# Feed-forward weights split by two chunks at a time, outer filter taps scaled on ScalarE, gates and splits for two row tiles at once

## The chip, the core and the metric

The kernel runs on one core of one Trainium2 chip. The core has a matrix engine (TensorE, PE in the profile, with its weight loads as PEld), a vector engine (VectorE, DVE), an engine for activations (ScalarE, ACT), a general engine (GpSimd, POOL) and a queue that issues most transfers (SyncE, SP). Each engine takes its instructions in order. The metric is the time of one execution on the device, in microseconds (us).

## The reference

A trunk of two layers on a sequence of 256 positions with 2048 channels, all in float32. Layer 0 mixes by pooling and attention, layer 1 by an mLSTM. Behind each mixer stands the same gated feed-forward block with 5632 hidden channels, and that block is what the change touches:

```python
def conv_ffn(x, w_up, conv_w, conv_b, w_down):
    u = x @ w_up
    up = jnp.pad(u, ((0, 0), (1, 1), (0, 0)))
    c = conv_w.astype(u.dtype)
    u = c[0] * up[:, :-2] + c[1] * up[:, 1:-1] + c[2] * up[:, 2:] + conv_b.astype(u.dtype)
    gate, val = jnp.split(u, 2, axis=-1)
    return (jax.nn.silu(gate) * val) @ w_down
```

The up product has 2 x 5632 output channels (gate and value), a filter of three taps runs over the positions, and SiLU of the gate times the value goes into the down product.

## The kernel before

**Weights.** Every weight matrix is cut on the host into chunks of 128 partitions by 1024 float32 values (512 KB). The program uses 890 chunks in one fixed order; `Stream` (from line 65) brings them in. `load` (line 82) takes a buffer `w` and issues the chunk's transfer on SP's queue. `split` (line 146) turns it into a pair of float32r values: a cast on ScalarE gives the high part (line 152), a subtraction on VectorE the low part (line 153), both into a buffer `hl`. Each float32 product is then three products of such parts (high x high, high x low, low x high). `ahead` (line 159) keeps loads and splits a set number of chunks in front of the matmuls: 5 and 2 outside the feed-forward blocks, 7 and 3 inside (line 1145), where there are 7 buffers `w` and 5 buffers `hl`. `next` hands out the chunk that the next matmuls use.

**Row tiles.** The 5632 hidden channels are 44 row tiles of 128, in groups of 4, 8, 8, 8, 8 and 8 (`FCH`). A row tile holds gate and value: 2 x 256 positions. Of each group of 8, the first four tiles (and all four of the group of 4) are made by `up` (line 969): four chunks, 16 matmuls each (8 with 512 and 8 with 256 columns). The other four tiles are a unit of `quads` (line 1019), which uses a scheme with fewer products (7 instead of 8 block products): 28 chunks of 6 matmuls (`p`), after which `finish` (line 1074) transposes the sums back (`tr`). The sums of weight blocks that the units need are either made in memory ahead of time by accumulating transfers from GpSimd (`make_step`, tiles `G`) or on VectorE (`sums` of `Stream`, lines 130 to 144).

**The tail of a row tile.** `tail` (line 953) works on gate and value in turn: ScalarE scales the middle tap and adds the bias (line 958), VectorE adds the outer taps with two multiply-adds (lines 959 and 961). Then SiLU on ScalarE (964), the product on VectorE (965), a cast on ScalarE (966) and a subtraction on VectorE (967) leave the split result in `g`, which is what the down product reads. Before that, `up` brings its two halves together (lines 432 and 433) and multiplies by the norm's factor (977); `finish` copies the transposes out (1083).

**Order.** TensorE's instructions stand in the program's order. `_ffn_plan` (line 1240) interleaves one chunk at a time: chunks of `up`, of `down` (line 1116, chunks of 12 matmuls `dn` of the group before), and of the units, spread over the places given in `UNITS`. The last group's `down` stands alone at the end of the layer, behind the `down` of the group before it. Small tasks (`finish`, the sums of activations, the norms) are put in between by `Weave`, which counts an estimated time at every group of matmuls. The other engines are ordered by a planner from dependencies.

Of the kernel before, what the change touches and what calls it, by code (L numbers as in the profile page):

```python
# [9 lines left out]
F32 = mybir.dt.float32  # L10
# [6 lines left out]
P = 128  # L17
# [46 lines left out]

class Stream:


    def __init__(self, tc, wpool, spool, dpool, srcs, make, load_ahead, split_ahead):
        self.tc, self.nc, self.wpool, self.spool, self.srcs = tc, tc.nc, wpool, spool, srcs
# [3 lines left out]
        self.more = None  # L73
        self.made, self.make, self.dpool = {}, make, dpool

    def home(self, i, raw):
        if self.more is None or i >= self.more[2]:
            return self.wpool if raw else self.spool
        return ((self.wpool if i % 7 < 6 else self.more[0]) if raw else
                (self.spool if i % 5 < 4 else self.more[1]))  # L80

    def load(self, pieces=1):
        i = self.n_load
        src = self.srcs[i]
        kind, src = src if isinstance(src, tuple) else ("plain", src)
        w = self.home(i, True).tile([P, CH * P], F32, tag="w", name=f"w{i}")
        if kind in ("made", "have"):
            width = n = CH * P
            at = 0
            for part in src:  # L90
                part = self.made[part[0]][:, part[1] * 512 : part[2] * 512] if isinstance(part, tuple) else part
                to = at + part.shape[-1]
                self.nc.sync.dma_start(w[:, at:to], part)
                at = to
        else:
            width = src.shape[-1]
            n = width // pieces
            for c in range(0, width, n):
                self.nc.sync.dma_start(w[:, c : c + n], src[:, c : c + n])
        self.w[i] = [w, n, width, kind, False]  # L100
        self.n_load += 1
        for step in self.make.pop(i, ()):
            self.make_step(*step)
# [26 lines left out]
    def sums(self, i):  # L130
        if i in self.w and not self.w[i][4] and self.w[i][3] not in ("plain", "made"):
            w, kind = self.w[i][0], self.w[i][3]
# [6 lines left out]
            if kind == "left":  # L139
                pin(add(l, l, r))  # L140
            if kind == "chain":
                pin(add(l, l, self.sum))
                pin(add(r, r, l))
            self.w[i][4] = True

    def split(self, then=None):
        i = self.n_split
        self.sums(i)
        w, n, width = self.w.pop(i)[:3]
        hl = self.home(i, False).tile([P, 2, CH * P], F32R, tag="hl", name=f"hl{i}")  # L150
        for c in range(0, width, n):
            (self.nc.vector.tensor_copy if i + c == 0 else self.nc.scalar.copy)(hl[:, 0, c : c + n], w[:, c : c + n])  # L152
            self.nc.vector.tensor_sub(hl[:, 1, c : c + n], w[:, c : c + n], hl[:, 0, c : c + n].bitcast(F32))  # L153
            then and then(c // n)
        self.hl[i] = hl
        self.n_split += 1
        self.sums(i + 1)

    def ahead(self, i, split=None):
        n = len(self.srcs)  # L160
        while self.n_load < min(n, i + self.la + 1):
            if self.n_load >= self.n_split + self.la - self.sa + 1:
                self.split()
            self.load()
        while self.n_split < min(n, i + (self.sa if split is None else split) + 1):
            self.split()

    def next(self):
        i = self.at
        self.ahead(i)  # L170
        self.at += 1
        return self.hl.pop(i)
# [48 lines left out]
def trunk(ctx: ExitStack, tc: tile.TileContext, gx, xT, xn, call, catt, cml, weights, make, out):  # L221
# [9 lines left out]
    wp = pool("wraw", 6)  # L231
    sp = pool("wsplit", 4)
# [705 lines left out]
    def ffn_layer(layer, norm, nxt):  # L938
        with ExitStack() as es:
# [4 lines left out]
            xsp = cp1 = lp(f"fs{layer}", 1)  # L944

# [7 lines left out]
            def tail(u, f, gt, i):  # L953

                y = tp.tile([P, 2, S], F32, tag="y", name=f"y{layer}_{f}")
                for j in range(2):
                    tl = f + j * FT
                    a.activation(y[:, j, :], u[:, j, :], AF.Identity, scale=cw(tl, 1), bias=cw(tl, 3))
                    v.scalar_tensor_tensor(y[:, j, 1:S], u[:, j, 0 : S - 1], cw(tl, 0), y[:, j, 1:S],
                                           ALU.mult, ALU.add)  # L960
                    v.scalar_tensor_tensor(y[:, j, 0 : S - 1], u[:, j, 1:S], cw(tl, 2), y[:, j, 0 : S - 1],
                                           ALU.mult, ALU.add)
                s_ = y[:, 0, :]
                a.activation(s_, s_, AF.Silu)
                v.tensor_mul(s_, s_, y[:, 1, :])
                a.copy(gt[:, i, 0, :], s_)
                v.tensor_sub(gt[:, i, 1, :], s_, gt[:, i, 0, :].bitcast(F32))

            def up(f, gt, i):
                ps = mmp.tile([P, 2, 2, S], F32, tag="mm", name=f"up{layer}_{f}")  # L970
                for q in range(KT // 4):
                    stat_part(ps, xx, list(range(4 * q, 4 * q + 4)), q == 0, q == KT // 4 - 1)
                    if q < KT // 4 - 1:
# [45 lines left out]
            def quads(fs, c, i0, name):  # L1019
# [9 lines left out]
                for p in range(m):  # L1029
# [9 lines left out]
                    yield  # L1039
# [12 lines left out]
                for p in range(m):  # L1052
# [8 lines left out]
                    yield  # L1061
                    if p % 2:
                        hl = st.next()
                        for n in range(2):
                            product(b1, block_of(2 * (p - 1 + n) + 1, 0), hl, n * 512, False, p - 1 + n == m - 1)
                        if p == m - 1:
                            c11 = part(11)
                            a.activation(c11, b1, AF.Copy, scale=r0)
                            gt = g_of(c)
                            wv.add(finish(c12, c22, fs[2:], gt, i0 + 2, name), 3.0)  # L1070
                            wv.add(finish(c11, c21, fs[:2], gt, i0, name), 11.0)
                        yield

            def finish(top, bottom, fs, gt, i0, name):

                for n, f in enumerate(fs):
# [7 lines left out]
                    tail(u, f, gt, i0 + n)  # L1084
# [31 lines left out]
            def down(c, gt, b):  # L1116
# [6 lines left out]
                for k in range(0, len(kts), 2):  # L1123
                    mov_part(ps, lambda k: gt[:, k], kts[k : k + 2], k == 0, k == len(kts) - 2)
                    if k < len(kts) - 2:
                        yield
# [18 lines left out]
            st.la, st.sa, st.more = 7, 3, (lp(f"fw{layer}", 1), lp(f"fh{layer}", 1), st.at + len(_ffn_plan(layer)))  # L1145
# [17 lines left out]
            st.la, st.sa, st.more = 5, 2, None  # L1163
# [61 lines left out]
def _down_chunks(w):  # L1225
# [9 lines left out]
    ((1, 1, 17, 38, 2), (2, 1, 45, 64, 2), (3, 1, 71, 100, 3), (4, 1, 107, 129, 2), (5, 1, 136, 158, 2)),  # L1235
    ((1, 1, 17, 39, 2), (2, 1, 46, 67, 2), (3, 1, 74, 97, 2), (4, 1, 104, 128, 2), (5, 1, 135, 157, 2)),
# [3 lines left out]
def _ffn_plan(layer):  # L1240

    slots = []
    for c, n in enumerate(FCH):
# [6 lines left out]
        for e in fill:  # L1250
            slots += [e] * (4 if e[0] == "n" else FCH[e[1]] // 2)
    here = [[] for _ in slots]
    m = KT // 2
    for c, h, lo, hi, kind in UNITS[layer]:
        one, two = 2 * m, m + m // 2
        long = 1.25 if kind == 3 else 1.0
        step = (hi - lo - 3) / (one * long + two)
        for k in range(one + two):
            at = k * long if k < one else one * long + k - one
            here[int(lo + at * step + (3 if k >= one else 0))].append(("s", c, h))  # L1260
# [3 lines left out]
    for b in range(NB):  # L1264
        plan += [("d", len(FCH) - 1, b)] * (FCH[-1] // 2)
    return plan

# [14 lines left out]
def _ffn_order(layer, up, dn, four, last):  # L1282
# [4 lines left out]
    for step in _ffn_plan(layer):  # L1287
        kind, c, i = step
        n = pos.get(step, 0)
        pos[step] = n + 1  # L1290
        if kind == "n":
            seq.append(up[(sum(FCH[:c]) + i) * 4 + n])
        elif kind == "d":
            seq.append(dn[d0[c] + i * (FCH[c] // 2) + n])
        else:
            u = [e[:2] for e in UNITS[layer]].index((c, i))
            made = UNITS[layer][u][4]
            if n >= 2 * m and (n - 2 * m) % 3 == 2:
                seq.append(last[u, (n - 2 * m) // 3])
                continue  # L1300
# [133 lines left out]
```

## Time and profile before

| | us |
|---|---|
| three runs | 2163.64, 2163.3, 2160.51 (median 2163.3) |
| the profiled execution, from its first to its last instruction | 2160.9 |
| attention layer | 0 to 266.8 |
| feed-forward of layer 0 | 266.8 to 973.0 |
| mLSTM layer | 973.0 to 1458.8 |
| feed-forward of layer 1 | 1458.8 to 2160.9 |

The stages overlap at their borders: the last down product of a layer begins while small work of the next is already under way, so the borders are those of TensorE's instructions to within a few matmuls. The clock granted to TensorE was 1.000 of full speed. In the profile's rows an engine and a line come first, then the operation, the tiles (written first, then read), the shapes, the count, busy time and mean duration; a group made by a helper carries the helper's line, so all matmuls have line 268 and are told apart by tile.

### The profile page before, as it was taken

The page shows a single profiled execution, that of the slowest core. Times are in us where ns is not written, and L with a number is a line of the kernel's source. Part 1 is how long each engine was busy: PE and PEld are TensorE (multiplying, and loading weights), DVE is VectorE, ACT ScalarE, POOL GpSimd, SP SyncE. Part 2 cuts the span into 40 slices and gives each one's busy share as a digit, 9 for nine tenths or more (in the row PEclk, how much of TensorE's full clock was granted, in tenths as well). Part 3 has the DMA queues.
Part 4 walks back from the last instruction along what each step waited for, and adds up shares of the span by engine and source line. Part 5 has one row for each costly group of instructions (what it writes and reads, how often), then busy time and mean ns, then how long its engine had stood idle before and what let it go on. Part 6 is the DMA issues. An engine that isn't in the chain of part 4 may idle for free.

```text
span 2160.9 us, 31049 instructions
## 1 busy us (share of the span) xinstructions
PE 2153.2 (100%) x10896; PEld 1826.7 (85%) x10896; DVE 1717.8 (79%) x2400; ACT 1309.2 (61%) x1840; POOL 276.0 (13%) x344
## 2 busy tenths in 40 slices
PE   9999999999999999999999999999999999999999
PEld 7888888888888888888888888888888888888887
DVE  7686698989889797866777677669898888879785
ACT  7665566766557576655454544556676666757663
POOL 0122111111111111111111111110000010000000
PEclk9999999999999999999999999999999999999999
DMA  8878899999999999979998998887999999877773
GB/s 325 257 229 246 256 262 345 316 332 320 308 325 308 351 332 339 319 200 250 250 263 251 256 253 244 258 244 223 312 286 306 302 297 288 272 249 238 259 245 119
DMA packets 204702, 596.15 MB, mean 276 GB/s; under 512 B 26010, under 2 KB 28354, under 8 KB 204546
## 3 DMA queue, kind: packets, MB, share of 16 engines
q1 hardware_dynamic: 167776, 531.43, 70.1%
q0 software_dynamic: 33696, 59.00, 18.3%
q10 hardware_dynamic: 3074, 3.75, 0.9%
q8 instruction: 85, 1.39, 0.2%
q14 instruction: 71, 0.58, 0.1%
HBM read 591.93 MB, written 119.58 MB: 329 GB/s over the span
## 4 chain that ended last, share of the span: by engine, by line
PE 93%; DMA 5%; DVE 1%; ACT 0%; issue 0%; SPq 0%; ACTq 0%; DVEq 0%
PE up L268 23%; PE dn L268 20%; PE p L268 16%; PE op L268 8%; PE mo L268 4%; PE mk L268 4%; PE mq L268 4%; PE mv L268 3%; PE qproj L268 3%; PE kproj L268 1%; PE vproj L268 1%; PE tr L1081 1%; DMA w<-G 1%; PE pool L268 1%; DMA w<-in_m_in 1%; DMA w<-in_up 1%
## 5 line engine op out<-in xcount | busy, mean ns | idle before, releaser
L153 DVE TENSOR_TENSOR hl<-w,hl 128x1024 fp32r<-128x1024 f32 (+2 forms) x892 | 1075.6, 1218 | 319.9 <-ACT hl L152 302.0
L152 ACT CAST hl<-w 128x1024 fp32r<-128x1024 f32 (+2 forms) x891 | 924.8, 1048 | 646.9 <-PE up L268 98.9
L268 PE MATMUL up<-xx,hl 128*128 128x512 f32 (+1 forms) x3072 | 560.2, 337 | 0.0
L268 PEld LDWEIGHTS up<-xx,hl 128*128 128x128 f32 x3072 | 486.7, 188 | 76.7
L268 PE MATMUL dn<-hl,g 128*128 128x512 f32 x2064 | 491.8, 391 | 0.0
L268 PEld LDWEIGHTS dn<-hl,g 128*128 128x128 f32 x2064 | 385.1, 188 | 79.0
L268 PE MATMUL p<-hl,sx 128*128 128x512 f32 x960 | 250.6, 390 | 0.0
L124 POOL DMA_DIRECT2D G<-in_q x160 | 132.0, 830 | 875.5 <-DMA G<-in_q 872.4
L268 PEld LDWEIGHTS p<-hl,sx 128*128 128x128 f32 x960 | 176.0, 188 | 34.4 <-DVE hl L153 0.6
L128 POOL DMA_DIRECT2D G<-G x144 | 127.9, 888 | 538.2 <-DMA G<-in_q 243.0
L268 PE MATMUL p<-hl,xx 128*128 128x512 f32 x720 | 193.5, 390 | 0.0
L268 PEld LDWEIGHTS p<-hl,xx 128*128 128x128 f32 x720 | 130.8, 188 | 24.0
L268 PE MATMUL mk<-xx,hl 128*128 128x512 f32 (+1 forms) x512 | 92.5, 338 | 1.4 <-DVE hl L153 1.4
L268 PE MATMUL mq<-xx,hl 128*128 128x512 f32 (+1 forms) x512 | 92.2, 337 | 0.0
L268 PE MATMUL mv<-hl,xx 128*128 128x512 f32 (+2 forms) x480 | 91.8, 350 | 0.0
L268 PE MATMUL op<-hl,cat 128*128 128x512 f32 x384 | 91.6, 393 | 0.0
L268 PE MATMUL mo<-hl,xx 128*128 128x512 f32 x384 | 90.5, 391 | 0.0
L268 PEld LDWEIGHTS mk<-xx,hl 128*128 128x128 f32 x512 | 79.0, 188 | 13.1 <-DVE hl L153 1.8
L268 PE MATMUL op<-hl,mcat 128*128 128x512 f32 x384 | 89.5, 392 | 0.0
L268 PEld LDWEIGHTS mq<-xx,hl 128*128 128x128 f32 x512 | 79.3, 188 | 11.6
L268 PEld LDWEIGHTS mv<-hl,xx 128*128 128x128 f32 x480 | 78.3, 189 | 11.2
L268 PEld LDWEIGHTS op<-hl,mcat 128*128 128x128 f32 x384 | 71.5, 188 | 14.6
(242 smaller groups left out, 1865.2 us busy)
## 6 DMA issues: line engine op xcount, KB each, us to landing
w<-in_up SPq DMA_DIRECT2D x192, 512.0 KB, 6.1
w<-in_dn SPq DMA_DIRECT2D x176, 512.0 KB, 6.2
w<-in_m_in SPq DMA_DIRECT2D x124, 512.0 KB, 6.0
w<-in_q SPq DMA_DIRECT2D x88, 512.0 KB, 6.2
G<-in_q SPq DMA_DIRECT2D x144, 256.0 KB, 6.4
G<-G POOLq DMA_DIRECT2D x144, 256.0 KB, 7.5
w<-G SPq DMA_DIRECT2D x72, 512.0 KB, 6.1
w<-in_a_in SPq DMA_DIRECT2D x46, 512.0 KB, 6.1
```

Of the source, the lines that this page charges most:

```text
L124: pin(add.dma_start(G[r, 0:512], src[r, 512:1024], accum_op=ALU.add))
L128: pin(add.dma_start(G[:, at : at + 512], G[:, of : of + 512], accum_op=ALU.add))
L152: (self.nc.vector.tensor_copy if i + c == 0 else self.nc.scalar.copy)(hl[:, 0, c : c + n], w[:, c : c + n])
L153: self.nc.vector.tensor_sub(hl[:, 1, c : c + n], w[:, c : c + n], hl[:, 0, c : c + n].bitcast(F32))
L268: pe.matmul(out_, lhsT, rhs, start=start, stop=stop, skip_group_check=True)
L1081: pe.transpose(tr[:, j, t * P : t * P + P], src[:, c : c + P], ident)
```

## The change

1. **Pairs of chunks.** Inside the feed-forward blocks, loads and splits handle two neighbouring chunks. The raw buffers are one tile with 6 slots (`Slots`), the split buffers one with 4; in the blocks 2 more of each are added, so 8 and 6 slots stand where there were 7 and 5 buffers. A pair takes two neighbouring slots. Where both chunks are halves of one stored block (up and down weights), one transfer of 1 MB brings both. One cast and one subtraction split the pair. Loads run 9 and splits 4 chunks ahead instead of 7 and 3.
2. **Order by two.** The plan interleaves two chunks at a time; the places in `UNITS` are halved with it.
3. **Taps.** The outer taps are scaled on ScalarE (four more activations per row tile), and added by two additions on VectorE that cover gate and value together.
4. **Gates by two.** SiLU, product, cast and subtraction run once for two row tiles.
5. **Memory.** The descriptor memory of GpSimd's transfers shrinks to 2048 bytes per partition.

```diff
+class Slots:
+    def both(self, j):
+        return self.parts[j // 100][:, j % 100 : j % 100 + 2]
...
+    def free(self, pair, extra):
+        n = [(100 * b, t.shape[1]) for b, t in enumerate(self.parts) if b == 0 or extra]
+        every = [o + k for o, m in n for k in range(0, m, 2 if pair else 1)]
+        free = [j for j in every if not self.busy.get(j) and not (pair and self.busy.get(j + 1))]
+        return min(free, default=None, key=lambda j: (
+            not pair and not self.busy.get(j ^ 1), max(self.age.get(j, -1), self.age.get(j + pair, -1)), j))
...
     def load(self, pieces=1):
...
+        if pair and got[0][0] == got[1][0] == "half" and got[0][1] is got[1][1] and got[0][2] == 0:
+            sync.dma_start(self.raw.both(j), got[0][1].rearrange("p (a n) -> p a n", a=2))
...
     def split(self, then=None):
...
+        if pair:
+            w, hl = self.raw.both(self.w[i][0]), self.hls.both(j)
+            self.nc.scalar.copy(hl[:, :, 0], w)
+            self.nc.vector.tensor_sub(hl[:, :, 1], w, hl[:, :, 0].bitcast(F32))
...
-            def tail(u, f, gt, i):
...
+            def taps(u, f, y):
+
+                t0 = sm1.tile([P, 2, S], F32, tag="sq", name=f"t0_{layer}_{f}")
                 for j in range(2):
                     tl = f + j * FT
...
+                    a.activation(y[:, j], u[:, j], AF.Identity, scale=cw(tl, 1), bias=cw(tl, 3))
+                    a.activation(t0[:, j], u[:, j], AF.Copy, scale=cw(tl, 0))
+                    a.activation(u[:, j], u[:, j], AF.Copy, scale=cw(tl, 2))
+                v.tensor_add(y[:, :, 1:S], y[:, :, 1:S], t0[:, :, 0 : S - 1])
+                v.tensor_add(y[:, :, 0 : S - 1], y[:, :, 0 : S - 1], u[:, :, 1:S])
+
+            def gates(y, gt, i):
+
+                s_, g = y[:, :, 0], gt[:, i : i + 2]
                 a.activation(s_, s_, AF.Silu)
...
+                v.tensor_mul(s_, s_, y[:, :, 1])
+                a.copy(g[:, :, 0], s_)
+                v.tensor_sub(g[:, :, 1], s_, g[:, :, 0].bitcast(F32))
+
+            def two(tag, f):
+                return cp1.tile([P, 2, 2, S], F32, tag=tag, name=f"{tag}{layer}_{f}")
...
-                tail(u, f, gt, i)
+                if i % 2 == 0:
+                    half[0] = two("yn", f)
+                taps(u, f, half[0][:, i % 2])
+                if i % 2:
+                    gates(half[0], gt, i - 1)
...
-                for k in range(0, len(kts), 2):
-                    mov_part(ps, lambda k: gt[:, k], kts[k : k + 2], k == 0, k == len(kts) - 2)
+                for k in range(0, len(kts), 4):
+                    mov_part(ps, lambda k: gt[:, k], kts[k : k + 4], k == 0, k == len(kts) - 4)
...
-            st.la, st.sa, st.more = 7, 3, (lp(f"fw{layer}", 1), lp(f"fh{layer}", 1), st.at + len(_ffn_plan(layer)))
+            st.raw.parts[1:] = [lp(f"fw{layer}", 1).tile([P, 2, CH * P], F32, tag="w", name=f"fw{layer}")]
+            st.hls.parts[1:] = [lp(f"fh{layer}", 1).tile([P, 2, 2, CH * P], F32R, tag="hl", name=f"fh{layer}")]
+            n = (st.n_load - st.at) % 2
+            st.la, st.sa, st.wide = 9, 4, (st.n_load + n, st.at + 2 * len(_ffn_plan(layer)))
...
-    ((1, 1, 17, 38, 2), (2, 1, 45, 64, 2), (3, 1, 71, 100, 3), (4, 1, 107, 129, 2), (5, 1, 136, 158, 2)),
-    ((1, 1, 17, 39, 2), (2, 1, 46, 67, 2), (3, 1, 74, 97, 2), (4, 1, 104, 128, 2), (5, 1, 135, 157, 2)),
+    ((1, 1, 8.5, 19, 2), (2, 1, 22.5, 32, 2), (3, 1, 35.5, 50, 3), (4, 1, 53.5, 64.5, 2), (5, 1, 68, 79, 2)),
+    ((1, 1, 8.5, 19.5, 2), (2, 1, 23, 33.5, 2), (3, 1, 37, 48.5, 2), (4, 1, 52, 64, 2), (5, 1, 67.5, 78.5, 2)),
...
+def _two(w):
+    return w.reshape(-1, 2, P, CH * P).transpose(0, 2, 1, 3).reshape(-1, P, 2 * CH * P)
...
+        arrays[f"up{l}"] = _two(_up_chunks(i["w_up"][l]))
+        arrays[f"dn{l}"] = _two(_down_chunks(i["w_down"][l]))
...
-    nc = _bacc.Bacc("TRN2", target_bir_lowering=False, num_devices=1)
+    nc = _bacc.Bacc("TRN2", target_bir_lowering=False, num_devices=1, dynamic_dma_scratch_size=2048)
```

More of the change, by code (lines that the diff above doesn't have):

```diff
@@ L72, in __init__ @@
         self.n_load = self.n_split = self.at = 0
-        self.more = None
+        self.wide = None
         self.made, self.make, self.dpool = {}, make, dpool
[L76 to L80, printed above, removed]
-    def load(self, pieces=1):
[L83 to L94, printed above, removed]
-        else:
[L96 to L103, printed above, removed]
@@ L130, in sums @@
     def sums(self, i):
-        if i in self.w and not self.w[i][4] and self.w[i][3] not in ("plain", "made"):
-            w, kind = self.w[i][0], self.w[i][3]
+        if i in self.w and not self.w[i][4] and self.w[i][3] in ("sum", "have", "left", "chain"):
+            j, kind, pair = self.w[i][0], self.w[i][3], self.w[i][5]
+            w = self.raw.at(j)
             l, r = w[:, 0:512], w[:, 512:1024]
@@ L147, in split @@
         i = self.n_split
[L148 to L157, printed above, removed]
+        pair = self.w[i][5]
+        j = self.hls.free(pair, self.extra(i))
+        if j is None:
+            return False
+        for k in range(1 + pair):
+            self.sums(i + k)
+        n, width = self.w[i][1:3]
+        self.hls.take(j, pair)
+        if pair:
+            w, hl = self.raw.both(self.w[i][0]), self.hls.both(j)
+            self.nc.scalar.copy(hl[:, :, 0], w)
+            self.nc.vector.tensor_sub(hl[:, :, 1], w, hl[:, :, 0].bitcast(F32))
+        else:
+            w, hl = self.raw.at(self.w[i][0]), self.hls.at(j)
+            for c in range(0, width, n):
+                (self.nc.vector.tensor_copy if i + c == 0 else self.nc.scalar.copy)(
+                    hl[:, 0, c : c + n], w[:, c : c + n])
+                self.nc.vector.tensor_sub(hl[:, 1, c : c + n], w[:, c : c + n], hl[:, 0, c : c + n].bitcast(F32))
+                then and then(c // n)
+        for k in range(1 + pair):
+            self.raw.give(self.w.pop(i + k)[0])
+            self.hl[i + k] = j + k
+            self.n_split += 1
+        for k in range(2):
+            self.sums(self.n_split + k)
+        return True
     def ahead(self, i, split=None):
@@ L1083, in finish @@
                     a.copy(u, tr)
-                    tail(u, f, gt, i0 + n)
+                    taps(u, f, y[:, n])
+                    if n:
+                        gates(y, gt, i0)
                     yield 4.0
```

135 lines of the change are left out of this document (93 added, 42 removed).

## The prediction

> **What bounds the kernel now.** I read the page's table of busy times first, then the stages, then who waited, then the chain.
>
> ```profile
> PE 2153.2 (100%) x10896; PEld 1826.7 (85%) x10896; DVE 1717.8 (79%) x2400; ACT 1309.2 (61%) x1840; POOL 276.0 (13%) x344
> ```
>
> TensorE is never idle by this line, but its ends are modelled, so the line alone is no proof. The view of stages (columns: stretch, its length, then busy us of each engine with its count, granted clock, DMA share, GB/s) has the two feed-forward stages and one stretch inside the first:
>
> ```profile
> core 0: us, PE busy (x) PEld busy (x) DVE busy (x) ACT busy (x) POOL busy (x), PEclk, DMA share, GB/s
> 266.80:973.00 706.20, 705.48 (x3519) 596.35 (x3518) 606.61 (x801) 452.72 (x598) 112.36 (x140) 1.00 0.99 311
> 1458.80:2160.90 702.10, 697.80 (x3461) 589.53 (x3459) 586.33 (x763) 437.02 (x565) 36.57 (x45) 1.00 0.82 261
> 688.00:776.00 88.00, 87.70 (x426) 73.68 (x424) 68.63 (x79) 51.39 (x59) 14.90 (x19) 1.00 1.04 345
> ```
>
> Together the two stages are 706.2 + 702.1 = 1408.3 us, at full granted clock. VectorE has 86% and 84% of them, ScalarE 64% and 62%, and in the first stage the DMA engines are full (0.99). What did TensorE's weight loads wait for, in the whole kernel?
>
> ```profile
> PEld mk L268 <- DVE hl L153: 1.8, 1, 1.8
> PEld wps L292 <- DVE x L287: 1.2, 1, 1.2
> PEld tr L1081 <- DVE c L1058: 0.9, 1, 0.9
> PEld p L268 <- DVE hl L153: 0.6, 2, 0.4
> ```
>
> Only `tr` and `p` are in the feed-forward stages: 0.9 + 0.6 = 1.5 us. That is the whole list of stalls which this change could remove there; behind each the next matmul is ready, so what goes is gained. Now the pace, from the chain of work (start, length, what), in stretches without a break:
>
> ```profile
> 1458.80 41.10 PE up L268 x236
> ```
> ```profile
> 2102.19 43.53 PE dn L268 x192
> ```
>
> One `dn` matmul (512 columns) takes 43.53/192 = 0.2267 us; one of `up` (512 and 256 columns in turn) 41.10/236 = 0.1742 us. With the counts of the groups
>
> ```profile
> L268 PE MATMUL dn<-hl,g 128*128 128x512 f32 x2064 | 491.8, 391 | 0.0
> L268 PE MATMUL up<-xx,hl 128*128 128x512 f32 x1536 | 483.6, 396 | 0.0
> L268 PE MATMUL up<-xx,hl 128*128 128x256 f32 x1536 | 302.1, 278 | 0.0
> L268 PE MATMUL p<-hl,sx 128*128 128x512 f32 x960 | 250.6, 390 | 0.0
> L268 PE MATMUL p<-hl,xx 128*128 128x512 f32 x720 | 193.5, 390 | 0.0
> ```
>
> the three products cost 2064 x 0.2267 + 3072 x 0.1742 + 1680 x 0.2267 = 467.9 + 535.1 + 380.9 = 1383.9 us of the 1408.3. The other 24 us hold the 48 matmuls `end` (10.9 us at this pace), the transposes, the first `mv` and the tail after the last matmul. **Both stages run at TensorE's own pace**, and the change leaves every matmul in place.
>
> [...]
>
> ```profile
> L268 PEld LDWEIGHTS dn<-hl,g 128*128 128x128 f32 x2064 | 385.1, 188 | 79.0
> ```
>
> **The change part by part.** *Splits.* Each layer's plan has 168 + 16 feed-forward chunks and 5 units of 28, that is 324; two layers make 648 chunks, 324 pairs. Today a chunk costs one cast on ScalarE and one subtraction on VectorE; half-size forms give the fixed part.
>
> ```profile
> L153 DVE TENSOR_TENSOR hl<-w,hl 128x1024 fp32r<-128x1024 f32 x882 | 1067.2, 1222 | 316.4 <-ACT hl L152 298.5 <-DMA G<-in_q 3.7 <-DMA w<-in_m_in 2.4
> L152 ACT CAST hl<-w 128x1024 fp32r<-128x1024 f32 x882 | 918.0, 1051 | 643.9 <-PE up L268 98.9 <-PE dn L268 93.2 <-DVE w L140 90.5
> ```
> ```profile
> L1001 ACT CAST sx<-v 128x512 fp32r<-128x512 f32 x16 | 9.7, 618 | 3.7 <-DVE v L992 3.7
> ```
> ```profile
> L433 DVE TENSOR_TENSOR tb_up<-up,tb_up x48: 680/686/694, 271.6 to 2104.5; 128x512 f32<-128x512 f32 x48
> ```
>
> ScalarE: 512 more elements cost 1051 - 618 = 433 ns, so a pair costs 1051 + 866 = 1917 ns instead of 2102: 185 saved. VectorE: 1222 - 686 = 536, so 1222 + 1072 = 2294 instead of 2444: 150 saved. Over 324 pairs: ScalarE -60 us, VectorE -49 us. (Both extrapolate beyond the widest row; no saving at all is the other end.)
>
> *Tails* (88 row tiles). The rows of the tile `y`, and one scaling on ScalarE as the new taps use it:
>
> ```profile
> L958 ACT ACTIVATE y<-tb_up,cst x96: 585/594/626, 278.2 to 2107.5; 128x256 f32<-128x256 f32 x96
> ```
> ```profile
> L961 DVE SCALAR_TENSOR_TENSOR y<-tb_up,cst,y x96: 473/479/484, 282.7 to 2111.4; 128x255 f32<-128x255 f32 x96
> L964 ACT ACTIVATE y<-y x88: 401/413/434, 285.2 to 2111.7; 128x256 f32<-128x256 f32 x88
> L965 DVE TENSOR_TENSOR y<-y x88: 410/419/429, 285.7 to 2113.2; 128x256 f32<-128x256 f32 x88
> L966 ACT CAST g<-y x88: 388/402/413, 287.5 to 2114.1; 128x256 fp32r<-128x256 f32 x88
> ```
> ```profile
> L557 ACT ACTIVATE pr<-pr,sm x24: 493/506/523, 72.7 to 177.0; 128x256 f32<-128x256 f32 x24
> ```
>
> ScalarE per tile now: 2 x 594 + 413 + 402 = 2003. After: 2 x 594 + 4 x 506 = 3212, plus half of a double SiLU and a double cast (about 620 each, by the 618 row), so 3832: +1829, over 88 tiles +161 us. VectorE now: 4 x 479 + 2 x 419 = 2754; after: two additions of 510 and half of two of 512 elements, 3 x 686 = 2058: -696, over 88 tiles -61 us. Totals: VectorE 1717.8 - 49 - 61 = 1608 (74%), ScalarE 1309.2 - 60 + 161 = 1410 (65%). Neither becomes the bound over the span; this exchange is worth nothing while TensorE hides both.
>
> *The split's delay.* The hl ring goes from five chunks to three pairs. In both, a slot is free four chunks before its next content is needed; product chunks (6 matmuls) are the shortest, 4 x 6 x 0.2267 = 5.4 us. A single split takes 1.05 + 1.22 = 2.3 us, a pair 1.92 + 2.29 = 4.2: worst room 1.2 us instead of 3.1. Positive, so nothing by itself; what queues ahead on the two engines decides. That is where two places matter.
>
> *Place one, the end of each layer.* `gates` now finishes two row tiles at once, and the last down product follows closely. From the timeline (start, length; last VectorE instruction of a row tile, and the `dn` stretch that reads it), first and second layer:
>
> ```profile
> 912.52 17.75 PE L268 MATMUL dn<-hl,g 128*128 128x512 f32 x77
> ```
> ```profile
> 927.32 0.42 DVE L967 TENSOR_TENSOR g<-y,g 128x256 fp32r<-128x256 f32 x1
> ```
> ```profile
> 2102.03 18.31 PE L268 MATMUL dn<-hl,g 128*128 128x512 f32 x80
> ```
> ```profile
> 2115.89 0.42 DVE L967 TENSOR_TENSOR g<-y,g 128x256 fp32r<-128x256 f32 x1
> ```
>
> Six matmuls read one row tile. In the second layer the last product starts 48 matmuls in; its tile k=2 is read at 2102.03 + 60 x 0.2267 = 2115.6, k=3 at 2117.0. The last tile is ready at 2116.3: 0.7 us to spare for k=3, but as a pair it must be there for k=2, 0.7 us earlier than today. In the first layer 6 matmuls precede the stretch; k=4 is read 66 matmuls after 912.52, at 927.5, and the last tile (k=5) is ready at 927.7. Who is busy before it?
>
> ```profile
> 896.90:927.70 30.80, 30.80 (x160) 26.17 (x159) 28.46 (x49) 21.86 (x36) 4.02 (x5) 1.00 0.93 270
> ```
>
> Five tails and about five pairs fall here: VectorE 28.5 - 5 x 0.70 - 5 x 0.15 = 24.2, ScalarE 21.9 + 5 x 1.83 - 5 x 0.19 = 30.1 of 30.8 us. ScalarE takes VectorE's place as the full engine exactly here. The shortest chain from the last `up` matmul is 0.6 + 2 x 0.69 + 3.2 + 2 x 0.69 + 0.62 + 0.69 + 0.62 + 0.69 = 9.2 us (evacuation, add, scale, taps, two additions, SiLU, product, cast, subtraction) against 13.6 us allowed; today's chain of 5.8 us took 14.3, so 8.5 us went to work in between. If that shrinks to 5, the stall is 0.6; if not, 9.2 + 8.5 - 13.6 = 4.1. I take 1.0 at each end, nearer the low side because VectorE, which is full today, is relieved: +2.0, bounds 0 to 8.2. It is a wait of a `dn` matmul, so the whole rest of TensorE's queue stands behind it and all of it reaches the end. The pair tiles `yn` and `yf` and the scratch `t0` have one buffer each, so a next pair's first scaling waits for the last `gates` of the pair before; splits queued behind it on ScalarE wait too. Pairs of one kind come over 10 us apart, so I add nothing.
>
> *Place two, full DMA* (688 to 776, share 1.04 above): there splits wait for landings.
>
> ```profile
> 760.87 2.36 DVE L153 TENSOR_TENSOR hl<-w,hl 128x1024 fp32r<-128x1024 f32 x2 [0.24 <-ACT hl L152]
> ```
> ```profile
> 762.34 1.52 PE L268 MATMUL p<-hl,sx 128*128 128x512 f32 x6
> ```
> ```profile
> 767.53 4.12 ACT L152 CAST hl<-w 128x1024 fp32r<-128x1024 f32 x4 [2.62 <-DMA w<-in_b]
> ```
>
> The first of these two subtractions ends near 762.1 and its matmuls start at 762.34, 0.25 us later. A pair delays its first chunk by 4.2 - 2.3 = 1.9 us, and by 512 KB more to land (1.5 us at 345 GB/s): 3.2 us late at most. Against it: the rings hold 8 + 6 instead of 7 + 5 chunks, 1 MB or 3.0 us more head start. I take +0.5, bounds 0 to 3.2.
>
> *The rest at nothing.* Up and down loads become 1 MB requests: half as many on SP's queue, same bytes, hidden while the rings are full. POOL gets a smaller descriptor memory; it is idle 87% of the span, and its sums are wanted many chunks later. If that cover went, the SP loads of the sums would be late and land in place two. The ring as one tile needs order kept by slot, not by tile; see the rivals.
>
> **Sum.** 2160.9 - 0.7 (about half of the 1.5 us goes) + 2.0 + 0.5 = 2162.7, on the span of the profiled execution. Nothing lies around that span that a run adds (one run took 2160.51), yet the median of the three is 2163.3, 2.4 above. I put the forecast half that offset higher: **2164 us**.
>
> **Rivals.** *ScalarE becomes the bound at each layer's end* (slower): the two waits reach 4 us each, 2164 - 2 + 8.2 = 2170. It decides from the point where the work between the chain's steps there stays above 13.6 - 9.2 = 4.4 us. For it: 30.1 of 30.8 us; against: VectorE's relief. [...] Chance 0.16.
>
> *Pairs come late where DMA is full* (slower): 3.2 us at 762, and as much at one or two more places: 2164 - 0.5 + 6.4 = 2170. Chance 0.10.
>
> *VectorE's relief or deeper rings free more* (faster): all 1.5 us and the 1.8 us of `mk` after the first layer go, and no new wait comes: 2160.9 - 3.3 = 2157.6, with the offset up to 2160. To pass 0.2% something must go that the wait view doesn't show. Chance 0.05. [...] Chance 0.01, in the same class.
>
> *The slots don't do what they say*: if order were kept for the whole tile, each pair would expose its 4.2 us: 2160.9 + 324 x 4.2 = 3520. Chance 0.02.
>
> **How the numbers follow.** The forecast (within 0.2%, 4.3 us, about what a measurement of this kernel can tell from no change) has 0.66. Slower: 0.16 + 0.10 + 0.02 = 0.28. Faster: 0.06. The range leaves out the two extreme cases and takes in both slower rivals with two us for the runs' spread, and the faster end: 2157 to 2173.
>
> **What would show it.** In the profile after: `hl` groups of 2048 elements near 1.92 us (ScalarE) and 2.29 us (VectorE); VectorE near 74%, ScalarE near 65%; stage lengths within 3 us of 706 and 702. The wait view shows `dn` waiting for `g` by a us or so near both layers' ends if place one is right, and none if VectorE's relief wins; a wait of `p` or `up` on `hl` near 760 if place two is right. I am wrong if TensorE's pace itself changes, or if waits on `hl` appear all over the stages.

## The result and the profile after

| | us |
|---|---|
| before, median of 4 runs (2160.05 to 2163.64) | 2161.91 |
| after, median of 4 runs (2273.82 to 2282.7) | 2279.98 |
| ratio, with its 95% interval | 1.0546 (1.0533 to 1.056) |
| profiled execution after, first to last instruction | 2278.4 |

The changed kernel is 118 us slower. The forecast was 2164, with a range that ended at 2173.

The page of the kernel after, busy times of the engines and then the two largest groups of pair splits (line, engine, operation, tiles, count; then busy us, mean ns; then idle time before them):

```profile
PE 2192.0 (96%) x10896; PEld 1844.2 (81%) x10896; DVE 1655.8 (73%) x1798; ACT 1386.3 (61%) x1786; POOL 276.8 (12%) x344
...
L209 DVE TENSOR_TENSOR hl<-w,hl 128x2048 fp32r<-128x2048 f32 x158 | 361.5, 2290 | 135.8 <-ACT hl L208 135.4
...
L208 ACT CAST hl<-w 128x2048 fp32r<-128x2048 f32 x158 | 301.3, 1909 | 187.4 <-PE up L339 69.6
```

The sizes that the prediction had put on the new instructions hold: a pair's cast takes 1909 ns (1917 expected), its subtraction 2290 (2294). No engine but TensorE is near full: VectorE has 73% of the span and ScalarE 61%. By the shares of busy time nothing has gone wrong, and yet TensorE now stands still for 4% of a longer span. Where? The view of stages (stretch and length; busy us of each engine with its count; granted clock, DMA share, GB/s), cut at TensorE's first matmul of the feed-forward, the mLSTM and the second feed-forward:

```profile
core 0: us, PE busy (x) PEld busy (x) DVE busy (x) ACT busy (x) POOL busy (x), PEclk, DMA share, GB/s
262.10:1037.80 775.70, 730.83 (x3547) 611.64 (x3546) 582.75 (x512) 495.13 (x577) 115.31 (x143) 0.97 0.93 286
1037.80:1525.00 487.20, 481.90 (x2572) 413.43 (x2571) 328.19 (x509) 243.28 (x337) 74.89 (x93) 1.00 0.88 248
1525.00:2273.60 748.60, 721.57 (x3523) 603.26 (x3521) 565.41 (x481) 485.96 (x552) 38.27 (x47) 0.99 0.76 247
```

Cut in the same way, the stages of the kernel before are 712.3, 479.7 and 708.0 us, and its attention 255.0 against 260.8 now. So the two feed-forward stages lose 63.4 and 40.6 us, and the two mixers, which the change was not to touch, 5.8 and 7.5. What TensorE waited for, in the whole kernel (us in total, times, longest):

```profile
PE dn L339 <- ACT g L1041: 28.6, 5, 10.2
PE p L339 <- DVE hl L209: 18.1, 11, 2.8
PE p L339 <- ACT tb L1167: 11.9, 4, 8.6
PE up L339 <- DVE xx L405: 5.7, 5, 1.9
PE tr_q L596 <- DVE rot_q L564: 3.2, 2, 3.0
PE p L339 <- DVE fh L209: 2.6, 1, 2.6
```

Two kinds of lateness fill this list. Split weights come late (`p` for `hl` and `fh`: 20.7 us). Row tiles come late: `dn` waits for `g` 28.6 us, and `p` for `tb`, the copy that takes finished transposes out of PSUM, 11.9 us. In the feed-forward stages of the kernel before, neither kind was above 0.6 us.

How can a row tile be 10 us late when no engine is full? The chain of work up to the longest stall, which ends at 744.97 (start, length, what):

```profile
736.09 4.47 DVE hl L209 x2
740.56 0.60 DVE yf L1034
...
742.53 0.60 ACT yn L1030
743.13 0.40 ACT t L1031
743.53 0.49 ACT yn L1030
744.01 0.40 ACT t L1031
744.41 0.52 ACT g L1041
...
744.97 7.16 PE dn L339 x18
```

The row tile's last addition of taps (`yf`, line 1034) stands in VectorE's queue behind two pair subtractions in a row, 4.47 us. By the timeline its input, a tap scaling that itself stood behind a pair's cast on ScalarE, is ready at 738.6; the addition starts at 740.5. The cast into `g` stands in ScalarE's queue behind four tap scalings of another row tile (`yn`, `t`), 1.9 us; its input is ready at 743.1, and it starts at 744.3. `dn` waits for that cast. Neither engine is full over the stage (VectorE 75% of its 775.7 us, ScalarE 64%); the work that matters is behind work that doesn't. The tails some 16 us earlier, in the timeline (the bracket is the idle time before an instruction and what ended it):

```profile
725.82 2.29 DVE L209 TENSOR_TENSOR hl<-fw,hl 128x2048 fp32r<-128x2048 f32 x1 [1.08 <-ACT hl L208]
...
728.03 0.69 DVE L1042 TENSOR_TENSOR g<-yf,g 128x512 fp32r<-128x512 f32 x1
...
728.75 2.09 ACT L1030 ACTIVATE yf<-tb,cst 128x256 f32<-128x256 f32 x4 [2.45 <-DVE g L1042]
```

`yf` has a single buffer. The subtraction that frees it, ready after the cast at 726.3, goes behind a pair subtraction until 728.03, and the scalings of the next pair, with all that follows them on ScalarE, wait 2.45 us for it.

**A second cost rides on the stalls.** The mean granted clock is 0.984 (1.000 before). At 0.50, which the view of stages has from 744.9 to 750.0, behind the longest stall, that is 2 x 0.016 x 2278 = 73 us, part of it idle. The next stages view has a stretch with a clock of 0.51 behind one stall and a stretch with 1.00 behind another, and the timeline of TensorE below it has the stalls themselves:

```profile
399.30:402.70 3.40, 3.31 (x8) 2.64 (x9) 3.40 (x5) 0.57 (x2) 0.82 (x1) 0.51 1.05 351
816.70:819.50 2.80, 2.78 (x12) 2.33 (x13) 2.71 (x2) 1.04 (x2) 1.64 (x2) 1.00 0.94 306
```
```profile
399.39 2.50 PE L339 MATMUL p<-hl,sx 128*128 128x512 f32 x5 [2.00 <-DVE hl L209]
...
816.72 2.79 PE L339 MATMUL p<-hl,sx 128*128 128x512 f32 x11 [2.61 <-DVE hl L209]
```

After 2.00 us of waiting, five matmuls took 2.50 us, at a clock of 0.51; after 2.61 us, eleven took 2.79, at 1.00. So the length of a wait alone does not tell which clock follows it; what else decides was not shown. Summed over the trace, starts of matmuls that lie over 0.3 us too far apart account for 95.0 us of lost time (6.2 before), which is 89 of the 118; the other 29 are smaller excesses, 23 of them between matmuls at a clock of 0.50.

### The profile page after: what moved, and what is told of

It reads as the page before. It is cut to its first block, busy times and chain, and to the rows that moved or that the text cites. A ratio compares the mean times of both kernels' runs of the same rounds, so it can differ in the third digit from the quotient of the medians.

```text
span 2278.4 us, 29440 instructions
## 1 busy us (share of the span) xinstructions
PE 2192.0 (96%) x10896; PEld 1844.2 (81%) x10896; DVE 1655.8 (73%) x1798; ACT 1386.3 (61%) x1786; POOL 276.8 (12%) x344
## 4 chain that ended last, share of the span: by engine, by line
PE 84%; DVE 6%; DMA 4%; ACT 4%; issue 2%; SPq 0%; POOL 0%; ACTq 0%; DVEq 0%
PE up L339 21%; PE dn L339 19%; PE p L339 14%; PE op L339 7%; PE mo L339 4%; PE mk L339 3%; PE mv L339 3%; PE mq L339 3%; DVE hl L209 3%; PE qproj L339 2%; ACT hl L208 1%; DMA w<-in_up 1%; PE pool L339 1%; PE kproj L339 1%; DMA G<-in_q 1%
## 5 line engine op out<-in xcount | busy, mean ns | idle before, releaser
L209 DVE TENSOR_TENSOR hl<-w,hl 128x2048 fp32r<-128x2048 f32 x158 | 361.5, 2290 | 135.8 <-ACT hl L208 135.4
L215 DVE TENSOR_TENSOR hl<-w,hl 128x1024 fp32r<-128x1024 f32 (+2 forms) x252 | 303.5, 1210 | 175.4 <-ACT hl L213 174.3
L213 ACT CAST hl<-w 128x1024 fp32r<-128x1024 f32 (+2 forms) x251 | 260.4, 1041 | 264.4 <-PE op L339 55.0
L208 ACT CAST hl<-w 128x2048 fp32r<-128x2048 f32 x158 | 301.3, 1909 | 187.4 <-PE up L339 69.6
L339 PE MATMUL up<-xx,hl 128*128 128x512 f32 (+1 forms) x1824 | 331.3, 338 | 0.4 <-DVE hl L215 0.4
L339 PEld LDWEIGHTS up<-xx,hl 128*128 128x128 f32 x1824 | 286.5, 189 | 44.5 <-DVE hl L215 0.8
L209 DVE TENSOR_TENSOR fh<-w,fh 128x2048 fp32r<-128x2048 f32 x80 | 183.2, 2290 | 73.2 <-ACT fh L208 68.2
L339 PE MATMUL up<-xx,fh 128*128 128x512 f32 x1248 | 228.9, 339 | 5.7 <-DVE xx L405 5.7
L339 PEld LDWEIGHTS up<-xx,fh 128*128 128x128 f32 x1248 | 196.8, 189 | 37.4 <-DVE xx L405 7.4
L208 ACT CAST fh<-w 128x2048 fp32r<-128x2048 f32 x80 | 152.7, 1909 | 110.9 <-PE dn L339 34.9
L339 PE MATMUL dn<-fh,g 128*128 128x512 f32 x648 | 166.7, 413 | 30.7 <-ACT g L1041 28.6
L209 DVE TENSOR_TENSOR hl<-fw,hl 128x2048 fp32r<-128x2048 f32 x54 | 123.6, 2290 | 48.6 <-ACT hl L208 48.5
L339 PEld LDWEIGHTS p<-hl,xx 128*128 128x128 f32 x504 | 93.9, 191 | 29.9 <-DVE hl L209 8.3
```

The costliest lines, as they stand in the source:

```text
L208: self.nc.scalar.copy(hl[:, :, 0], w)
L209: self.nc.vector.tensor_sub(hl[:, :, 1], w, hl[:, :, 0].bitcast(F32))
L339: pe.matmul(out_, lhsT, rhs, start=start, stop=stop, skip_group_check=True)
```

## The experiments

The theory on the pairs: their cast and subtraction hold ScalarE and VectorE for 1.9 and 2.3 us, so the first chunk of a pair and everything queued behind it come late. Its rivals: the new tail (taps on ScalarE, gates by two) makes the row tiles late; loads by pairs or the slots make the weights late; or it is the plan by two or the smaller descriptor memory.

### One part undone at a time

**Single splits.** Loads, slots and splits take one chunk again.

```diff
 def pair(self, i):
-    return bool(self.wide and ...)
+    return False
```

> The changed kernel with every split and load of one chunk again; slots, order by two, taps on ScalarE and gates by two stay. Theory A (row tiles come late: taps on ScalarE and gates by two) expects the waits of dn for g (32 us in the changed kernel) and for tb (12 us) to stay, and a time of 2235 to 2260. Theory B (pairs of splits come late) expects the waits of p for hl (21 us) to vanish, ScalarE to be free in shorter steps, and a time of 2165 to 2200. Theory C (the slots and the order by two) expects 2260 or more.

Measured: 2218.9, ratio to before 1.0262 (1.0233 to 1.0292), 61 us below the changed kernel. `p` no longer appears with `hl` among the long waits (one wait of 3.0 us for `fh` is left); `dn` still waits 9.5 us for `g` and `p` 5.6 for `tb`.

**Taps back on VectorE**, as multiply-adds (gates still by two).

```diff
-    a.activation(t0[:, j], u[:, j], AF.Copy, scale=cw(tl, 0))
-    a.activation(u[:, j], u[:, j], AF.Copy, scale=cw(tl, 2))
-v.tensor_add(y[:, :, 1:S], y[:, :, 1:S], t0[:, :, 0 : S - 1])
...
+    v.scalar_tensor_tensor(y[:, j, 1:S], u[:, j, 0 : S - 1], cw(tl, 0), y[:, j, 1:S],
+                           ALU.mult, ALU.add)
...
```

> The changed kernel with the outer taps as multiply-adds on VectorE again; pairs and gates by two stay. Theory A expects most of the waits for g and tb to go if the scaling on ScalarE is what makes row tiles late: 2200 to 2230; near 2270 if the gates by two are. Theory B expects 2250 to 2285, since VectorE has 61 us more and splits wait for it.

Measured: 2250.24, 1.0407 (1.0369 to 1.0446). `dn` for `g` falls from 28.6 to 16.4 us, `p` for `hl` is 20.2 (18.1 with the whole change).

**Gates for each row tile** (taps still on ScalarE).

```diff
-if i % 2:
-    gates(half[0], gt, i - 1)
+gates(y, gt, i)
...
```

> The changed kernel with SiLU, product, cast and subtraction for each row tile by itself and two buffers for it; pairs and scaling on ScalarE stay. Theory A expects 2200 to 2240 if the joint gates and their single buffer make row tiles late. Theory B expects 2250 to 2285.

Measured: 2267.27, 1.0486 (1.0447 to 1.0526).

**The whole old tail**, both edits above together.

> The changed kernel with the whole tail of a row tile as before the change; pairs of splits, slots and order by two stay. Theory A expects waits for g and tb near nothing and 2190 to 2215 (the waits of p for hl, 21 us, and what the clock loses after them stay). Theory B expects 2240 or more.

Measured: 2241.74, 1.0368 (1.0338 to 1.0398). `dn` still waits 17.0 us for `g`, `p` 16.2 for `hl`. So the row tiles come late even with the tail of before; in the next kernel, which has no pairs either, this wait is gone.

### Both parts, and the length of an instruction

**Old tail and single splits.**

> The changed kernel with the old tail and single splits and loads together; left of the change are the slots, the order by two and the smaller descriptor memory. If the tail (about 38 us by itself) and the pairs (61 us by themselves) add up, 2280 - 61 - 38 = 2181; if both work through the same wait, 2195 to 2215. Theory C expects what is left over 2162 to be in the order by two and the slots: waits for g in the feed-forward stages and 5 us each in attention and mLSTM.

Measured: 2204.92, 1.0204 (1.0147 to 1.0261). 43 us stay although neither part is left. In this setting the parts don't add up: single splits alone took off 61 us and the old tail alone 38, but both together 75.

**Pairs as they are, but in small steps:** loads and slots by pairs, each split as two casts and two subtractions of 1024 elements (new tail kept).

```diff
-self.nc.scalar.copy(hl[:, :, 0], w)
-self.nc.vector.tensor_sub(hl[:, :, 1], w, hl[:, :, 0].bitcast(F32))
+for k in range(2):
+    self.nc.scalar.copy(hl[:, k, 0], w[:, k])
+    self.nc.vector.tensor_sub(hl[:, k, 1], w[:, k], hl[:, k, 0].bitcast(F32))
```

> The changed kernel, but each pair is split by two casts and two subtractions of one chunk each; loads, slots and lookahead stay by pairs. If the length of the single instruction is what delays the tails and the splits behind it (grain), this falls most of the way to the kernel with single splits: 2215 to 2235. If slots and landings by pairs are (a pair begins only when both slots are free and both chunks have landed), it stays at 2260 to 2285.

Measured: 2212.76, 1.024 (1.0211 to 1.027), 67 us below the changed kernel, with the same transfers, slots and order. `p` waits for `hl` no more. So the length of the instructions takes the largest share, and loads by pairs, which this kernel keeps, do not.

### The 43 us that stay

**Order by one** on top of the old tail and single splits, so that of the change only slots, deeper look-ahead and descriptor memory are left.

```diff
-slots += [e] * (2 if e[0] == "n" else FCH[e[1]] // 4)
+slots += [e] * (4 if e[0] == "n" else FCH[e[1]] // 2)
...
```

> The kernel with old tail and single splits, and the plan again by one chunk: left are the slots, the deeper lookahead and the smaller descriptor memory. If the order by two costs what is left in the feed-forward stages, these fall to 712 and 708 us and the total to 2165 to 2175; if the slots do, it stays where the run with the order by two is.

Measured: 2195.3, 1.016 (1.011 to 1.021). Most of the 43 us is still there; the 10 us between this kernel and the one before it lie within the spread of their runs (two each, 9 and 10 us apart).

**The descriptor memory alone**, in the kernel before.

```diff
-nc = _bacc.Bacc("TRN2", target_bir_lowering=False, num_devices=1)
+nc = _bacc.Bacc("TRN2", target_bir_lowering=False, num_devices=1, dynamic_dma_scratch_size=2048)
```

> The kernel before with the smaller descriptor memory alone. All theories: no change, 2158 to 2166; over 2170 would mean that GpSimd's transfers are held up by it.

Measured: 2161.62, 1.0006 (0.9995 to 1.0018). Nothing. That leaves the slots and the deeper look-ahead; of the two, only the slots reach into the mixers, which had become slower too. A single chunk doesn't take the slot that has been free longest: it first takes one whose neighbour is busy, to keep whole pairs free, and that can be one freed a moment ago. The mixers, which work in single chunks alone, showed it. Timeline of the kernel with order by one, in the attention:

```profile
57.22 1.05 ACT L213 CAST hl<-w 128x1024 fp32r<-128x1024 f32 x1 [5.31 <-DMA w<-in_a_in]
```

A cast waits 5.31 us for its weights to land. Its queue of loads (waits of SP's queue there):

```profile
SPq L141 <- DMA w<-in_a_in: 6.5, 1, 6.5
```

A load is held for 6.5 us, by this view, by an earlier one that has not landed. So the next kernel takes out that preference.

**Oldest slot**, else the same as the kernel with order by one.

```diff
-    not pair and not self.busy.get(j ^ 1), max(self.age.get(j, -1), self.age.get(j + pair, -1)), j))
+    max(self.age.get(j, -1), self.age.get(j + pair, -1)), j))
```

> The kernel with old tail, single splits and the plan by one chunk, and one more edit: a single chunk takes the slot that has been free longest, where the changed kernel prefers a slot whose neighbour is busy. Theory D (that preference takes a slot that was given back only just, so a load or a cast waits for the split or the matmuls of the chunk just before it, while an older slot stands empty) expects the whole 34 us to go: 2158 to 2168. If the one tile instead of a pool costs them in another way, 2185 to 2200.

Measured: 2166.54, 1.0021 (1.0012 to 1.0031): some 29 us go with one term of a sort key. The 5.31 us wait is gone from its trace.

**The same line in the changed kernel.**

> The whole change with the oldest free slot. Pairs choose by age already, so theory D expects gains in attention, mLSTM and at the borders alone: 5 us in attention, 5 to 8 in mLSTM, some 3 at each feed-forward start, 2260 to 2270. Without theory D 2275 to 2285.

Measured: 2264.8, 1.048 (1.0464 to 1.0495): 15 us below the changed kernel. Attention and mLSTM are back at 255.4 and 478.1 us, the feed-forward stages stay at 773.0 and 749.0.

### The parts again, without that disturbance

All kernels from here on take the oldest slot. Three cases: new tail with single splits, old tail with pairs, old tail with single splits (order by two in all).

> The oldest free slot, with single splits and loads; new tail and order by two stay. It shows what the tail and the order by two cost without pairs and without the slots' choice. If the pairs are the cause behind both kinds of wait (on hl and on g), 2162 to 2172; if scaling on ScalarE and gates by two cost by themselves, 2180 to 2200 with waits for g.

> The oldest free slot, with pairs and the old tail. It shows what the pairs cost by themselves: waits of p for hl and of dn for g, 2215 to 2230 if the effects add up; below 2180 if pairs cost little without the new tail.

> Oldest free slot, old tail, single splits and loads, order by two: only the order is new against the run with the oldest slot and the plan by one chunk (2166.5). If the order by two is innocent, 2163 to 2172; if it carries part of the 28 us of the new tail (2195 with single splits), 2175 to 2190.

| us (ratio to before, interval) | pairs in one step | single splits |
|---|---|---|
| new tail | 2264.8 | 2195.26 (1.0157, 1.0142 to 1.0173) |
| old tail | 2235.02 (1.0344, 1.0325 to 1.0362) | 2165.37 (1.0018, 1.0009 to 1.0027) |

Read by rows, pairs cost 69.5 us with the new tail and 69.7 with the old one; by columns, the new tail costs 29.8 and 29.9. With neither, order by two stands within about a us of order by one (2165.37 and 2166.54). With the new tail and single splits (first fence), and with the old tail and pairs (second), TensorE waits:

```profile
PE dn L339 <- ACT g L1041: 12.2, 5, 3.1
PE p L339 <- ACT tb L1167: 4.4, 1, 4.4
```
```profile
PE p L339 <- DVE hl L209: 18.1, 9, 2.8
PE dn L339 <- ACT g L1040: 17.1, 6, 5.9
PE p L339 <- ACT tb L1163: 5.0, 4, 2.5
```

The new tail delays row tiles alone. Pairs delay weights and, more in sum (22.1 us), the row tiles too.

**Loads and slots by pairs, splits in small steps, old tail.**

> Oldest free slot, old tail, pairs of loads and slots, but each pair split in steps of one chunk. If the length of the instructions is the whole cost of the pairs (2235 with long ones), this is within 3 us of the run with single splits and loads, 2162 to 2172, and the only version that might reach the kernel before with half the load requests; if landings or slots by pairs cost something, 2180 or more. None expects it clearly under 2158.

Measured: 2165.12, 1.0019 (1.0009 to 1.003), the same as with single chunks throughout. Requests of 1 MB instead of 512 KB, pair slots and landing by pairs cost nothing and bring nothing that these runs can tell. Busy times on its page, and below them those of the old tail with pairs in one step:

```profile
PE 2155.3 (99%) x10896; PEld 1828.1 (84%) x10896; DVE 1713.1 (79%) x2378; ACT 1312.3 (61%) x1840; POOL 276.9 (13%) x344
```
```profile
PE 2178.4 (98%) x10896; PEld 1838.6 (82%) x10896; DVE 1689.9 (76%) x2060; ACT 1260.0 (56%) x1522; POOL 277.4 (12%) x344
```

The kernel that is 70 us slower has 23 us less work on VectorE and 52 us less on ScalarE. Its only difference is that each two casts became one, and each two subtractions. Fewer instructions (2060 for 2378 on VectorE, 1522 for 1840 on ScalarE) and less work go with a longer time of the kernel.

**The tail's two edits, one by one, on that kernel.** First gates by two, then scaling on ScalarE (gates each).

> The run with small steps, with gates by two added (taps on VectorE). If the joint gates make the row tiles late (28 us for the whole new tail), 2180 to 2195 with waits of dn for g; if the scaling does, 2163 to 2175.

> The run with small steps, with the outer taps scaled on ScalarE (gates for each tile by itself). If the scaling makes the row tiles late, 2180 to 2195; if the gates by two do, 2163 to 2175. Both may share it.

Measured: gates by two 2170.06, 1.004 (1.0027 to 1.0054), scaling 2178.13, 1.0079 (1.0062 to 1.0097), so +5 and +13 us. Together they were +30, 12 more than the sum. With scaling alone `dn` already waits:

```profile
PE dn L340 <- ACT g L1042: 6.3, 4, 2.3
...
PE dn L340 <- DVE g L1043: 1.7, 3, 0.8
```

Both edits lengthen the same chain from the last product to `g`, so the second starts with no room left. That this makes up the whole 12 us was not measured.

**Long cast, short subtractions**, to see which of the two long instructions it is.

```diff
+self.nc.scalar.copy(hl[:, :, 0], w)
 for k in range(2):
-    self.nc.scalar.copy(hl[:, k, 0], w[:, k])
     self.nc.vector.tensor_sub(hl[:, k, 1], w[:, k], hl[:, k, 0].bitcast(F32))
```

> Oldest free slot, old tail, pairs, the cast as one instruction of 2048 and the subtraction as two of 1024. If both long instructions hold up the chain alike, about half of the 65 to 70 us of the pairs stays: 2195 to 2210. If the long subtraction on VectorE, the fuller engine, is the cause, 2170 to 2185; if the long cast is, 2220 to 2235.

Measured: 2231.36, 1.0329 (1.0312 to 1.0347). Of the 70 us, 66 are there with the long cast alone. Its waits:

```profile
PE dn L340 <- ACT g L1041: 21.0, 6, 6.1
PE p L340 <- DVE hl L210: 9.0, 10, 1.8
PE p L340 <- ACT tb L1164: 5.9, 4, 2.5
```

Short subtractions halve the wait for weights (18.1 to 9.0 us), but 3.9 us come back as `dn` waiting for `g` and the rest in smaller waits: the eight longest lines of this view add up to 47.6 us in both kernels, with and without the short subtractions. The long subtraction with short casts was not tried, so what it costs by itself is open.

## Why the prediction was wrong

**What held.** TensorE was the bound and nothing was to be gained: no version here beats the kernel before, and the two best that keep more of the change than its descriptor memory, at 2165, are 4 us above it. What the chance of faster counts beside its 0.05, another 0.01, no run shows. The durations of every new instruction held. Summed over the trace, VectorE's instructions shrank by 114 us (the prediction's terms: 110) and ScalarE's grew by 96 (101). The totals of 1608 and 1410 us weren't reached (1655.8 and 1386.3): busy time on a page counts overlapping instructions once (1655.8 for 1744.9 us of durations on VectorE, 1386.3 for 1500.8 on ScalarE), and the prediction took sums of durations from it. Place two, the stretch with full DMA, has one wait of `p` for `hl`, the 2.61 us at 816.72, inside the bounds of 0 to 3.2. Its cause was another: the chain of work before it holds no landing, only casts and VectorE's work, with another pair's subtraction ahead of the one that is waited for. With small steps the wait is gone, so loads by pairs cost nothing.

Place one came true where it was forecast. The last product of each layer waits for `g`, where the prediction had looked:

```profile
991.66 5.34 PE L339 MATMUL dn<-fh,g 128*128 128x512 f32 x12 [4.87 <-ACT g L1041]
...
2230.37 5.49 PE L339 MATMUL dn<-fh,g 128*128 128x512 f32 x12 [5.64 <-ACT g L1041]
```

That is 10.5 us for the 2.0 taken (bounds 0 to 8.2 for both ends), and 6.9 us with the new tail and single splits. The rival "ScalarE becomes the bound at each layer's end", at 4 us for each end, was right in place, mechanism and nearly in price. It missed the result because the layer ends are two of many such places.

**What failed, in the order of its size.**

1. *"worst room 1.2 us instead of 3.1. Positive, so nothing by itself"*. This term was set to 0 and measured 70 us. The 4.2 us of a pair were taken as two instructions that run when their turn comes. The clause after it, "what queues ahead on the two engines decides", named the cause, but it was then applied at two places only. With 1.2 us of room, another pair's cast (1.9 us) or three tap scalings (0.5 us each) ahead of a cast are enough to make a weight late; and the other way round, each 1.9 us cast is ahead of some step of a tail. The test for a split's own delay cannot see that second half, which is the larger one in the waits (22.1 of 40.2 us with pairs and the old tail).

2. *"This exchange is worth nothing while TensorE hides both"* (taps and gates), with +2.0 at the layer ends. Measured +30 us. The prediction asked whether an engine is full over the span and then looked at the two ends of the layers for a tight hand-off. It is tight at other groups too: with the new tail and single splits, the two ends hold 6.9 of the 14.6 us that `dn` waits for the parts of `g`. This is the first group of the kernel before, in its timeline:

```profile
325.27 0.42 DVE L967 TENSOR_TENSOR g<-y,g 128x256 fp32r<-128x256 f32 x1
...
325.52 2.66 PE L268 MATMUL dn<-hl,g 128*128 128x512 f32 x11
```

The last row tile is ready at 325.69, and the stretch reads it 6 matmuls in, at 325.52 + 6 x 0.2267 = 326.9: 1.2 us to spare. After the change, with pairs and new tail, the same group has a stall of 4.0 us there:

```profile
339.45 5.46 PE L339 MATMUL dn<-fh,g 128*128 128x512 f32 x12 [3.96 <-ACT g L1041]
```

3. *"Pairs of one kind come over 10 us apart, so I add nothing"* (single buffers `yn`, `yf`, `t0`). They are not apart when the pair before is late itself: ScalarE waited 2.45 us for `yf` at 728.75. How much of the 30 us this is was not measured by itself.

4. *"The rest at nothing"*, with order kept by slot. Measured 15 us, and 29 in the version without pairs. The rival on slots had the right place with the wrong mechanism: order is kept by slot, as meant, but the choice of the slot brings a new load behind work that has just begun. The prediction counted the added slots as head start and put no price on the sort key.

5. No step allowed for the clock. A stall was priced at its own length. Some 23 of the 118 us are the wider spacing of matmuls at a clock of 0.50 behind stalls.

The sum by the runs: 4 (order, look-ahead and slots, old tail and single splits) + 70 (pairs in one step) + 30 (tail) + 15 (choice of slot) = 119 for the 118 measured. These are steps from one kernel to the next, so they add up in any case; what makes them prices of the parts is that pairs and tail cost the same with and without each other in the table above.

**What stays open.** Why the planner puts whole casts and tap scalings ahead of the steps that TensorE waits for: its estimates don't show in a trace. What a long subtraction costs with short casts. And what decides whether a clock of 0.5 follows a wait, as after the 2.00 us that ended at 399.39, or does not, as after the 2.61 us that ended at 816.72.

## What to carry to other kernels

An engine that is 60% busy can still be late: here, with ScalarE at 61% and VectorE at 73%, an addition that was ready at 738.6 started at 740.5, behind two pair subtractions of 4.47 us together. The length of each instruction was latency for what queued behind it, and two instructions merged into one made hand-offs late (70 us, with 23 us less work on VectorE and 52 less on ScalarE). That such a merger gains time where the engine is the bound was not shown. Before such a change, list the room at every hand-off to the bound engine (ready time against read time), not only where an engine is full, and count the new instruction's length against each. When buffers become slots picked by hand, pick the one free longest, and look for the cost in the stages that the change does not touch.

## What the runs showed of the hardware that was not expected

One wait of TensorE cost more than itself: after 2.00 us of it the granted clock was 0.51 from 399.3 to 402.7, and five matmuls of 512 columns took 2.50 us where eleven took 2.79 at a clock of 1.00. A longer wait, of 2.61 us, was followed by a clock of 1.00 from 816.7 to 819.5. Requests of 1 MB instead of 512 KB made no difference to the time (2165.12 against 2165.37 us).
